# SSD mixer: a chunk's new state from three products of split factors, with the tiles' places shared anew

## The chip, the cores and the metric

The kernel runs on one core of a Trainium2 chip. The metric is the device time of one execution in microseconds. Shown are the median of three runs and, apart from it, one execution that the hardware profiler recorded.

## The reference

One inference step of a two-layer encoder over 512 prompt tokens (one stream) and 8 running streams of 16 tokens, 640 tokens in all, with 1024 channels. Layer 0 is FFN, a mixer of S5 and stick-breaking attention, FFN; layer 1 is FFN, the Mamba-2 SSD mixer, FFN. The change lies in the SSD mixer. Its recurrence, for each of 4 groups of 8 heads (64 channels a head, 128 states), runs over chunks of tokens:

```python
def step(h, inp):
    x_c, dt_c, b_c, c_c = inp
    cs = jnp.cumsum(dt_c * a, axis=1)
    ...
    y = jnp.einsum('btsgr,bsgrp->btgrp', w, x_c)
    y = y + jnp.einsum('btgn,bgrpn->btgrp', c_c, h) * jnp.exp(cs)[..., None]
    to_end = jnp.exp(cs[:, -1:] - cs) * dt_c
    h_new = h * jnp.exp(cs[:, -1])[..., None, None] + jnp.einsum('bsgr,bsgn,bsgrp->bgrpn', to_end, b_c, x_c)
    return h_new, y
```

The last einsum, the sum over a chunk's tokens of B times the scaled x, is the product that the change rewrites. The prompt's state starts at zero; the running streams bring their states with them (`ssd_h0`).

## The kernel before

All is float32 in memory. The big products are made from operands split in two: `split` (lines 99 to 101) casts a value on ScalarE to the type fp32r (the high part) and subtracts that from the value on VectorE (the low part); `mm3` (140 to 148) then sums high x high, low x high and high x low, three fp32r matmuls in place of one. Line 146 is that matmul for most of the kernel. A matmul whose operands are plain float32 shows as two records in the trace.

The SSD mixer (`mixer1`) first projects group 0, then takes 20 steps: 4 groups g, in each the chunks c = 4, 0, 1, 2, 3. Chunk 4 holds the eight running streams; chunks 0 to 3 are 128 prompt tokens each. One turn of the loop at lines 1842 to 1850 issues: one unit of the next group's projections (`run_fill`, line-146 matmuls), `core_a` of the next step, `core_b` (c < 4) or `core_s` (c = 4) of this step, perhaps one more unit, and `gate_out` of the group before.

- `core_a` (1658 to 1719) loads the chunk's B, C and x (`bx`, line 1660, two places) and the running sums (`csb`, 1665), makes the decay weights, transposes B into `bk` (1692, 1698) and x (1701), and scales the transposed x by head: `xe` (factor to the chunk's end) and `xd` (time step), eight ScalarE multiplications each at line 1709 (in group 3, `xd` in one VectorE instruction, 1705). For c = 4 it also splits `xe` and `bk` into `xs_` (a place of `h0`, or of `og` in group 0) and `bs_`, and writes both to DRAM (`xb_d`, 1717 and 1718) for use in the last FFN.
- `core_b` (1721 to 1754): the old state's part (1727), the state product `pst` from `bk` and `xe` (1731), the new state `hst` (1736, 1737), the chunk's own part (1745), and `y` (1749 to 1752). Line 1752 is the last reader of `bx`.
- `core_s` (1756 to 1780): for the running streams, the chunk's own part (1764); then four blocks j of two streams each: `load_h0` (1454 to 1457) brings 512 KB of states, and two matmuls (1769) write 32 rows of the bank `pi`. `xe` is reused for the sum of both (1771, 1772), which is transposed (1775) and finished at 1778, there the last reader of `bx`. Tiles `h0` have four places, and group 0's four loads are issued long before (1825, list `ahead`).

Each tile name has as many places as its `bufs`; a new tile of that name waits until the last reader of the oldest is done. All loads and stores named here are issued by SyncE's queue (SP), in its order. The order on each engine is fixed when the kernel is built: a planner takes the program's order as priority and lets a later instruction pass one that is not ready in its own estimate of times, so that loads and matmuls of a later part can stand ahead of an earlier one in the trace. The trace leaves the numbers out of names: `h0` is `h` there, and all PSUM tiles are `bank`.

Of the kernel before, what the change touches and what calls it, by code (L numbers as in the profile page):

```python
# [10 lines left out]
F32 = mybir.dt.float32  # L11
F32R = mybir.dt.float32r
# [10 lines left out]
T = 640  # L23
# [14 lines left out]
def kernel(ctx: ExitStack, tc: tile.TileContext, I, O, phases=PHASES):  # L38
    nc = tc.nc
# [59 lines left out]
    def split(hi, lo, src):  # L99
        nc.scalar.copy(hi, src)  # L100
        return nc.vector.tensor_tensor(lo, src, hi.bitcast(F32), op=ALU.subtract)  # L101
# [1350 lines left out]
    ssd = {}  # L1452

    def load_h0(wk, g, j):
        h0 = wk.tile([128, 2, 512], F32, name="h0", bufs=4)
        nc.sync.dma_start(h0, I["ssd_h0"][g, 2 * j:2 * j + 2].rearrange("b n c -> n b c"))
        return h0

# [38 lines left out]
    def mixer1(ph, last):  # L1497
# [4 lines left out]
        xb_d = ssd["xb"] = [dram.tile([2, 128, 640], F32, name=f"xb_d{g}") for g in range(4)]  # L1502
        z_d = [dram.tile([128, NT, 4, 128], F32, name=f"z_d{g}") for g in range(4)]
        with ExitStack() as st:
# [105 lines left out]
            nc.sync.dma_start(dr[:, 0:256], I["m1_dt"])  # L1610
            split(dtw[:, 0, 0:256], dtw[:, 1, 0:256], dr[:, 0:256])
            tok = wk.tile([128, NT, 3, 32], F32, name="tok")
            dt, cs = (wk.tile([32, T], F32, name=n) for n in ("dt", "cs"))
            rst, te = (wk.tile([128, 1024], F32, name="csb", bufs=2)[:32, :T] for _ in range(2))
            with after_norm():
                V.memset(rst, 1.0)
# [38 lines left out]
            bl = {}  # L1655
            ahead = []

            def core_a(g, c):
                bx = wk.tile([128, 6, 128], F32, name="bx", bufs=2)
                nc.sync.dma_start(bx, bcx_d[g][:, c])  # L1660
                bt, ct, xs = bx[:, 0], bx[:, 1], bx[:, 2:6]
                hs = slice(8 * g, 8 * g + 8)
                off = lambda r: cs_d[r:r + 1, 128 * c:128 * c + 128].offset
                csb = wk.tile([128, 1024], F32, name="csb", bufs=2).rearrange("p (h t) -> p h t", t=128)
                nc.sync.dma_start(csb, bass.AP(tensor=cs_d.tensor, offset=off(8 * g), ap=[[0, 128], [T, 8], [1, 128]]))

                el = None
                if c < 4:
                    el = small.tile([128, 8], F32, name="el")
                    nc.scalar.activation(el, csb[:, :, 127], AF.Exp)  # L1670
                else:
                    e8 = wk.tile([128, 8, 8], F32, name="e8")
                    nc.scalar.activation(e8.rearrange("p b h -> p h b"),
                                         csb.rearrange("p h (b i) -> p h b i", i=16)[:, :, :, 15], AF.Exp)
                    nc.sync.dma_start(el_d[:, g], e8.rearrange("p b h -> p (b h)"))
                ecs = None
                if 0 < c < 4:
                    ecs = wk.tile([128, 4, 128], F32, name="ecs", bufs=1)
                    for h in range(2):
                        nc.sync.dma_start(ecs[64 * h:64 * h + 64],  # L1680
                                          bass.AP(tensor=cs_d.tensor, offset=off(8 * g + h),
                                                  ap=[[0, 64], [2 * T, 4], [1, 128]]))
                    nc.scalar.activation(ecs, ecs, AF.Exp)
                elif c == 4:
                    ecs = wk.tile([128, 8], F32, name="ecs8")
                    nc.scalar.activation(ecs, tok[:, c, 0, hs], AF.Exp)
                V.tensor_tensor(csb, csb, tok[:, c, 0, hs, None].to_broadcast([128, 8, 128]), op=ALU.subtract)
                nc.scalar.activation(csb, csb, AF.Relu, scale=-1.0)
                nc.scalar.activation(csb, csb, AF.Exp, scale=-1.0)
                pcb = bank_b()  # L1690
                nc.tensor.matmul(pcb[:, 0:128], bt, ct, start=True, stop=True)
                nc.tensor.transpose(pcb[:, 128:256], bt, ident)
                cbm = wk.tile([128, 128], F32, name="cbm", bufs=2)
                V.tensor_tensor(cbm, pcb[:, 0:128], mc[:, c // 4, :], op=ALU.mult)
                V.tensor_tensor(csb, csb, cbm[:, None, :].to_broadcast([128, 8, 128]), op=ALU.mult)

                bk = wk.tile([128, 128], F32, name="bk", bufs=2)
                nc.scalar.copy(bk, pcb[:, 128:256])
                px = bank_b()
                for q in range(4):  # L1700
                    nc.tensor.transpose(px[:, 128 * q:128 * q + 128], xs[:, q], ident)
                xd, xe = (wk.tile([128, 512], F32, name=n, bufs=2) for n in ("xd", "xe"))
                for o, k in ((xe, 2), (xd, 1)):
                    if g == 3 and k == 1:
                        V.tensor_tensor(by_head(o), by_head(px), tok[:, c, k, hs, None].to_broadcast(hb3), op=ALU.mult)
                    else:
                        for h in range(8):
                            d = slice(64 * h, 64 * h + 64)
                            nc.scalar.mul(o[:, d], px[:, d], tok[:, c, k, 8 * g + h:8 * g + h + 1])
                if c == 4:  # L1710

                    xs_ = (wk.tile([128, 2, 512], F32R, name="h0", bufs=4) if g else
                           wk.tile([128, 4, 2, 128], F32R, name="og", bufs=1).rearrange("p (a q) k c -> p a (q k c)", a=2))
                    bs_ = wk.tile([128, 2, 128], F32R, name="bs", bufs=1)
                    split(xs_[:, 0], xs_[:, 1], xe)
                    split(bs_[:, 0], bs_[:, 1], bk)
                    nc.sync.dma_start(xb_d[g][:, :, 0:512].rearrange("a t c -> t a c"), xs_.bitcast(F32))
                    nc.sync.dma_start(xb_d[g][:, :, 512:640].rearrange("a t c -> t a c"), bs_.bitcast(F32))
                bl[g, c] = ct, xs, csb, el, ecs, bk, xd, xe

            def core_b(g, c):
                ct, xs, csb, el, ecs, bk, xd, xe = bl.pop((g, c))

                if c:
                    pi = bank_b().rearrange("p (q t) -> p q t", t=128)
                    for q in range(4):
                        nc.tensor.matmul(pi[:, q, :], hst[g][:, 128 * q:128 * q + 128], ct,
                                         start=(q == 0), stop=(q == 3), skip_group_check=True)

                pst = bank_b()  # L1730
                nc.tensor.matmul(pst, bk, xe, start=True, stop=True)
                hn = wk.tile([128, 512], F32, name="hst", bufs=2)
                if c == 0:
                    nc.scalar.copy(hn, pst)
                else:
                    G.tensor_tensor(by_head(hn), by_head(hst[g]), el[:, :, None].to_broadcast(hb3), op=ALU.mult)
                    V.tensor_tensor(hn, hn, pst, op=ALU.add)
                hst[g] = hn
                if c == 3:
                    nc.sync.dma_start(O["ssd_p"][g], hn)  # L1740

                pw = bank_b().rearrange("p (q t) -> p q t", t=128)
                for q in range(4):
                    for h in range(2):
                        nc.tensor.matmul(pw[64 * h:64 * h + 64, q, :], xd[:, 128 * q + 64 * h:128 * q + 64 * h + 64],
                                         csb[:, 2 * q + h, :], start=(q == 0), stop=(q == 3), skip_group_check=True)
                y = wk.tile([128, 4, 128], F32, name="yb", bufs=6)
                if c:
                    V.tensor_tensor(y, pi, ecs, op=ALU.mult)
                    V.tensor_tensor(y, y, pw, op=ALU.add)  # L1750
                for q in range(4):
                    V.scalar_tensor_tensor(y[:, q, :], xs[:, q], chp[:, 0, 4 * g + q:4 * g + q + 1],
                                           y[:, q, :] if c else pw[:, q, :], op0=ALU.mult, op1=ALU.add)
                ys[g, c] = y

            def core_s(g, c):

                ct, xs, csb, el, ecs, _, xd, xe = bl.pop((g, c))
                c4 = ct.rearrange("p (j q i) -> p j q i", q=2, i=16)
                for q in range(2):  # L1760
                    G.tensor_copy(ctm[:, q, :, q, :], c4[:, :, q, :])
# [90 lines left out]
            for c in range(NT):  # L1852
                gate_out(3, c)
                if c == 0:
                    g_bc = [wk.tile([128, 2, 512], F32, name="h0", bufs=4).rearrange("p a b -> p (a b)")
                            for _ in range(2)]
                    load_gb(LN_OF[ph], g_bc)
                layer_norm(c, g_bc, last)
                if c >= 2:
                    run_pend()  # L1860
# [159 lines left out]
```

## Time and profile before

| | |
|---|---|
| median of 3 runs | 2525.61 us (2523.7 to 2527.52) |
| profiled execution, own time | 2531.27 us |
| its span, first to last instruction | 2529.6 us |
| mean granted TensorE clock | 0.995 of full |
| busy: TensorE, VectorE, ScalarE, GpSimd | 2490.1, 2014.5, 1269.2, 373.5 us |
| line 1731, the state product | 16 products, 32 records, 594 ns each |
| line 1769, the running streams' states | 64 records in 4 steps |

The recurrence of the SSD mixer spans about 1660 to 2050 us of the trace. The page gives busy time by engine, and the views of groups of instructions (by line and shape), of waits (who waited for whom), of stretches of time and of single engines in order of time give the rest. Busy shares of TensorE overstate its work, since matmuls overlap: a group's time from its first start to the next group's start is what it costs. In the view in order of time a row gives the start, the length from first start to last end, the engine, line and operation, and the number of instructions merged; a bracket gives the idle time before it and what ended that.

### The profile page before, as it was taken

How to read it: one execution, taken by the hardware profiler on the slowest of the kernel's cores; microseconds unless marked ns; L12 is line 12 of the kernel's file. 1: busy time of each engine (PE TensorE's matmuls, PEld its weight loads, DVE VectorE, ACT ScalarE, POOL GpSimd, SP SyncE). 2: the span in 40 equal slices, each digit the busy share in tenths (PEclk: the TensorE clock that was granted, in tenths of full speed). 3: DMA queues.
4: the chain of work that ended last, by engine and by line, in shares of the span. 5: the costliest groups of instructions: out<-in, count | busy, mean ns of one | idle time of the engine just before them, and what ended most of it. 6: DMA issues, size and time to landing. Idle time of an engine off the chain costs nothing. (4 is left out here: it accounts for less than half of the span.)

```text
span 2529.6 us, 40802 instructions
## 1 busy us (share of the span) xinstructions
PE 2490.1 (98%) x15551; PEld 2286.1 (90%) x15551; DVE 2014.5 (80%) x3505; ACT 1269.2 (50%) x2389; POOL 373.5 (15%) x492
## 2 busy tenths in 40 slices
PE   9999999999999999999999999999999999999998
PEld 8999999878789999999999999998999879999897
DVE  7788777676879888877988887787575789998887
ACT  4444344336744555553555554566465543554542
POOL 0000001210130000013000002311121152111121
PEclk9999999999999999999999999999999999999999
DMA  5332335443222433452144434556464723555563
GB/s 186 109 100 78 116 112 161 144 150 117 87 79 64 119 102 97 112 164 66 59 114 113 120 100 132 158 162 204 137 211 137 242 74 99 154 151 165 151 172 116
DMA packets 179253, 324.80 MB, mean 128 GB/s; under 512 B 21312, under 2 KB 92608, under 8 KB 178544
## 3 DMA queue, kind: packets, MB, share of 16 engines
q1 hardware_dynamic: 165200, 293.83, 36.9%
q0 software_dynamic: 13856, 28.35, 5.8%
q8 instruction: 122, 2.00, 0.3%
q14 instruction: 75, 0.61, 0.1%
HBM read 259.56 MB, written 40.54 MB: 119 GB/s over the span
## 5 line engine op out<-in xcount | busy, mean ns | idle before, releaser
L100 ACT CAST w<-raw 128x512 fp32r<-128x512 f32 (+1 forms) x721 | 532.7, 769 | 337.3 <-DVE raw L349 144.7
L101 DVE TENSOR_TENSOR w<-raw,w 128x512 fp32r<-128x512 f32 (+2 forms) x721 | 621.2, 883 | 86.9 <-ACT w L100 84.0
L366 PE MATMUL bank<-xhi,w 128*128 128x320 f32 x2432 | 436.2, 309 | 2.3 <-DVE s L408 1.4
L366 PE MATMUL bank<-T,w 128*128 128x320 f32 x2736 | 428.2, 310 | 5.3 <-ACT bank L383 2.7
L366 PEld LDWEIGHTS bank<-T,w 128*128 128x128 f32 x2736 | 406.8, 188 | 8.6 <-ACT bank L383 5.3
L366 PEld LDWEIGHTS bank<-xhi,w 128*128 128x128 f32 x2432 | 376.8, 188 | 6.6 <-DVE s L408 2.2
L146 PE MATMUL bank<-xhi,w 128*128 128x256 f32 (+2 forms) x2272 | 364.3, 312 | 5.2 <-ACT xhi L100 2.6
L146 PEld LDWEIGHTS bank<-xhi,w 128*128 128x128 f32 x2272 | 337.3, 189 | 15.8 <-issue 4.9
L146 PE MATMUL bank<-w,h 128*128 128x512 f32 x1488 | 346.5, 391 | 0.2 <-DVE yacc L223 0.2
L146 PEld LDWEIGHTS bank<-w,h 128*128 128x128 f32 x1488 | 277.2, 188 | 57.9 <-ACT h L100 1.6
L366 PE MATMUL bank<-xlo,w 128*128 128x320 f32 x1216 | 227.8, 309 | 0.0
L349 DVE TENSOR_TENSOR raw<-raw 128x512 f32<-128x512 f32 x304 | 214.0, 704 | 3.4
L366 PEld LDWEIGHTS bank<-xlo,w 128*128 128x128 f32 x1216 | 190.8, 188 | 0.0
L146 PE MATMUL bank<-xlo,w 128*128 128x256 f32 (+2 forms) x1136 | 190.0, 309 | 0.0
L515 POOL DMA_DIRECT2D yacc<-ev x84 | 72.6, 893 | 690.2 <-ACT ev L514 619.8
L146 PEld LDWEIGHTS bank<-xlo,w 128*128 128x128 f32 x1136 | 171.6, 188 | 0.6
L502 PE MATMUL bank<-w,h 128*128 128x512 f32 x576 | 134.5, 390 | 0.0
L502 PEld LDWEIGHTS bank<-w,h 128*128 128x128 f32 x576 | 107.9, 188 | 22.7 <-DVE yacc L511 0.2
L379 ACT COPY mx<-bank 128x320 f32<-128x320 f32 x152 | 64.6, 425 | 105.9 <-PE bank L366 105.2
L223 DVE SCALAR_TENSOR_TENSOR yacc<-bank,yacc 128x512 f32<-128x512 f32 x120 | 82.0, 687 | 40.3 <-PE bank L146 39.7
L511 DVE SCALAR_TENSOR_TENSOR yacc<-bank,yacc 128x512 f32<-128x512 f32 x84 | 57.8, 688 | 67.4 <-PE bank L502 67.4
L146 PE MATMUL bank<-w,og 128*128 128x512 f32 x432 | 103.1, 394 | 0.0
(437 smaller groups left out, 3359.0 us busy)
## 6 DMA issues: line engine op xcount, KB each, us to landing
raw<-in_w_gate_dram SPq DMA_DIRECT2D x88, 512.0 KB, 3.7
raw<-in_w_up_dram SPq DMA_DIRECT2D x88, 512.0 KB, 3.8
raw<-in_w_down_dram SPq DMA_DIRECT2D x88, 512.0 KB, 3.6
raw<-in_m_in_dram SPq DMA_DIRECT2D x52, 512.0 KB, 4.6
yacc<-ev POOLq DMA_DIRECT2D x84, 256.0 KB, 4.7
raw<-in_m_out_dram SPq DMA_DIRECT2D x24, 512.0 KB, 4.3
csb<-cs_d SPq DMA_DIRECT2D x20, 512.0 KB, 5.3
h<-in_ssd_h_dram SPq DMA_DIRECT2D x16, 512.0 KB, 6.6
```

The lines of the kernel that those rows point to most:

```text
L100: nc.scalar.copy(hi, src)
L101: return nc.vector.tensor_tensor(lo, src, hi.bitcast(F32), op=ALU.subtract)
L146: state["pe"] = nc.tensor.matmul(ps, a, b, start=(k == 0), stop=(k == n - 1)).ins
L223: state["acc"] = nc.vector.scalar_tensor_tensor(ya, pb, scale, ya, op0=ALU.mult, op1=ALU.add).ins
L349: V.tensor_tensor(o, v, w, op=ALU.subtract)
L366: nc.tensor.matmul(ps, A[p][:, a, k * 128:k * 128 + 128], X[p][b][:, k, :], start=(first and n == 0), stop=(n == 11), skip_group_check=True)
L379: nc.scalar.copy(e[n], ps)
L502: nc.tensor.matmul(ps, a[:, u], b[:, v], start=(first and n == 0), stop=(n == 5), skip_group_check=True)
L511: V.scalar_tensor_tensor(ya, ps, 0.5 / ALPHA, ya, op0=ALU.mult, op1=ALU.add)
L515: nc.gpsimd.dma_start(yacc[:, t, 512 * j:512 * j + 512], e, accum_op=ALU.add)
```

## The change

The state product's factors are split for every chunk, and line 1731 becomes three fp32r matmuls into the same bank: high x high, high x low, low x high. `bk` and `xe` hold both parts; `xe` is first made whole in a new tile `xr` with one place, split, and only then is `xd` made. For c = 4 the parts that exist now go to DRAM, and `xs_` and `bs_` go. `core_s` takes `xr` for the sum that it kept in `xe`. To make room, `h0` has three places, not four, and `dt`, used only ahead of the loop, lies in the place of `og`.

```diff
     def load_h0(wk, g, j):
-        h0 = wk.tile([128, 2, 512], F32, name="h0", bufs=4)
+        h0 = wk.tile([128, 2, 512], F32, name="h0", bufs=3)
...
-            dt, cs = (wk.tile([32, T], F32, name=n) for n in ("dt", "cs"))
+            dt = wk.tile([128, 4, 2, 128], F32, name="og", bufs=1).rearrange("p q k c -> p (q k c)")[:32, :T]
+            cs = wk.tile([32, T], F32, name="cs")
...
-                bk = wk.tile([128, 128], F32, name="bk", bufs=2)
-                nc.scalar.copy(bk, pcb[:, 128:256])
+                bk = wk.tile([128, 2, 128], F32R, name="bk", bufs=2)
+                split(bk[:, 0], bk[:, 1], pcb[:, 128:256])
...
-                xd, xe = (wk.tile([128, 512], F32, name=n, bufs=2) for n in ("xd", "xe"))
-                for o, k in ((xe, 2), (xd, 1)):
+                xd = wk.tile([128, 512], F32, name="xd", bufs=2)
+                xr = wk.tile([128, 512], F32, name="xr", bufs=1)
+                xe = wk.tile([128, 2, 512], F32R, name="xe", bufs=2)
+                for o, k in ((xr, 2), (xd, 1)):
...
+                    if k == 2:
+                        split(xe[:, 0], xe[:, 1], xr)
                 if c == 4:
-
-                    xs_ = (wk.tile([128, 2, 512], F32R, name="h0", bufs=4) if g else
-                           wk.tile([128, 4, 2, 128], F32R, name="og", bufs=1).rearrange("p (a q) k c -> p a (q k c)", a=2))
-                    bs_ = wk.tile([128, 2, 128], F32R, name="bs", bufs=1)
-                    split(xs_[:, 0], xs_[:, 1], xe)
-                    split(bs_[:, 0], bs_[:, 1], bk)
-                    nc.sync.dma_start(xb_d[g][:, :, 0:512].rearrange("a t c -> t a c"), xs_.bitcast(F32))
-                    nc.sync.dma_start(xb_d[g][:, :, 512:640].rearrange("a t c -> t a c"), bs_.bitcast(F32))
+                    nc.sync.dma_start(xb_d[g][:, :, 0:512].rearrange("a t c -> t a c"), xe.bitcast(F32))
+                    nc.sync.dma_start(xb_d[g][:, :, 512:640].rearrange("a t c -> t a c"), bk.bitcast(F32))
...
                 pst = bank_b()
-                nc.tensor.matmul(pst, bk, xe, start=True, stop=True)
+                for n, (a, b) in enumerate(((0, 0), (0, 1), (1, 0))):
+                    nc.tensor.matmul(pst, bk[:, a], xe[:, b], start=(n == 0), stop=(n == 2))
...
-                ct, xs, csb, el, ecs, _, xd, xe = bl.pop((g, c))
+                ct, xs, csb, el, ecs, _, xd, _ = bl.pop((g, c))
+                xe = wk.tile([128, 512], F32, name="xr", bufs=1)
...
-                    g_bc = [wk.tile([128, 2, 512], F32, name="h0", bufs=4).rearrange("p a b -> p (a b)")
+                    g_bc = [wk.tile([128, 2, 512], F32, name="h0", bufs=3).rearrange("p a b -> p (a b)")
```

## The prediction

> **What bounds the kernel now.** I read the page first, then the stretches of time, then TensorE's waits in the SSD mixer, then the mixer's engines in order of time.
>
> ```profile
> PE 2490.1 (98%) x15551; PEld 2286.1 (90%) x15551; DVE 2014.5 (80%) x3505; ACT 1269.2 (50%) x2389; POOL 373.5 (15%) x492
> ```
>
> ```profile
> 1650.00:2050.00 400.00, 394.69 (x2615) 356.93 (x2615) 285.15 (x485) 234.14 (x622) 77.59 (x149) 0.99 0.57 176
> 1756.00:1759.50 3.50, 1.08 (x7) 0.76 (x5) 2.69 (x4) 1.75 (x4) 0.00 (x0) 1.00 0.95 288
> 1759.50:1769.70 10.20, 10.12 (x46) 7.10 (x47) 6.09 (x9) 5.84 (x23) 0.51 (x4) 0.50 0.65 203
> ```
>
> The columns of the stretches are its length, the busy time of TensorE, its weight loads, VectorE, ScalarE and GpSimd, then the granted clock, DMA's share and GB/s. TensorE is busy for 394.69 of the mixer's 400 us; VectorE for 285.15 (71%) and ScalarE for 234.14 (59%). So what lengthens or shortens TensorE's stream counts in full, and work on the other two counts only where TensorE waits for it. The other two rows show the worst such place: TensorE stood still from 1757.08 (1755.53 + 1.55, below) to 1759.58, and the next 10.2 us were granted half the clock.
>
> ```profile
> 1755.53 1.55 PE L146 MATMUL bank<-xlo,w 128*128 128x384 f32 x8
> 1759.58 0.77 PE L1691 MATMUL bank<-bx 128*128 128x128 f32 x2 [2.50 <-DMA bx<-bcx_d]
> ...
> 2020.69 0.46 PE L1691 MATMUL bank<-bx 128*128 128x128 f32 x2 [0.67 <-DMA bx<-bcx_d]
> ...
> 2031.82 0.49 PE L1691 MATMUL bank<-bx 128*128 128x128 f32 x2 [0.39 <-DMA bx<-bcx_d]
> ```
>
> That place costs 2.5 us of waiting and half of 10.2, 5.1 us: 7.6 us. With the two waits at the end these are all three of TensorE's waits for `bx` in 20 loads; the other 17 steps had it in time.
>
> **The change part by part.** *The state product.* In the views by shape (busy us, mean ns) and in order of time:
>
> ```profile
> L146 PE MATMUL bank<-w,og 128*128 128x512 f32 x384 | 91.7, 394 | 0.0
> ...
> L1731 PE MATMUL bank<-xe,bk 128*128 128x512 f32 x32 | 16.4, 594 | 0.0
> ```
>
> ```profile
> 2012.09 1.02 PE L1731 MATMUL bank<-xe,bk 128*128 128x512 f32 x2
> ...
> 2014.31 5.71 PE L146 MATMUL bank<-w,og 128*128 128x512 f32 x24
> ...
> 2026.76 1.02 PE L1731 MATMUL bank<-xe,bk 128*128 128x512 f32 x2
> 2027.46 3.97 PE L146 MATMUL bank<-w,og 128*128 128x512 f32 x16
> ```
>
> One product is two records of 594 ns in 1.02 us together, so the second starts 0.43 us after the first and the pair takes 0.86 us of the stream. The new matmuls have the type and shape of the 24 at 2014.31; without the last one's own 0.39 us the other 23 starts fill 5.32 us, (5.71 - 0.39)/23 = 0.231 us each (the group of 16: (3.97 - 0.39)/15 = 0.239), their weight loads included. Three take 0.69 us. Over 16 products: 16 x (0.86 - 0.69) = **-2.7 us** (-2.3 with 0.239). A switch between types seems to cost nothing: at 2026.76 a plain product stands between fp32r matmuls, and the next starts 0.70 us on, not later than 0.86.
>
> The Trainium skill, "TensorE: Matmul & The Clock Gate", section "Back-to-back issue gap", gives about 131 ns for each 512-column matmul in a sustained stream; by it three would take 0.39 us and the change save 7.5 us, an estimate. The rows here disagree, with 231 to 239 ns, and the measurement decides.
>
> *The fourth `h0` load.* This is the part that I think matters most. Four blocks of the running streams' states used to have four places. With three, the fourth block's load can start only when the first block's matmuls are done.
>
> ```profile
> 1671.55 1.94 PE L1769 MATMUL bank<-h,ctm 128*32 128x512 f32 x16
> 1673.43 2.10 PE L146 MATMUL bank<-xhi,w 128*128 128x256 f32 x16
> 1675.36 1.07 PE L146 MATMUL bank<-xlo,w 128*128 128x256 f32 x8
> 1676.27 0.33 PE L146 MATMUL bank<-xhi,w 128*128 128x384 f32 x1
> 1676.44 0.60 PE L1775 MATMUL bank<-ident,xe 128*128 128x128 f32 x4
> 1676.80 2.85 PE L146 MATMUL bank<-xhi,w 128*128 128x384 f32 x15
> ```
>
> ```profile
> 1671.55 0.18 PEld L1769 LDWEIGHTS bank<-h,ctm 128*32 128x32 f32 x8
> 1672.01 0.15 PEld L1769 LDWEIGHTS bank<-h,ctm 128*32 128x32 f32 x4 [0.28 <-issue]
> 1672.44 0.15 PEld L1769 LDWEIGHTS bank<-h,ctm 128*32 128x32 f32 x4 [0.28 <-issue]
> ```
>
> Sixteen records of 512 columns, 4 for each block, go through in 1.88 us (1671.55 to 1673.43): the weight loads come in fours, 0.43 us apart, so the four blocks, each 32 columns wide, run side by side in four steps. If the fourth must come later, the first three still take four steps and so does the fourth alone: 1.88 us more (four bare steps, 1.72, at least), in each of 4 groups: **+7.5 us** (6.9 at least; 0 if the planner found a way to keep them together, which a place still in use seems to exclude). A fill of projections follows, so the fourth block has something to stand behind, as the transposes at 1676.44 stand inside a group of line 146.
>
> ```profile
> L1456 SPq DMA_DIRECT2D h<-in_ssd_h_dram x16: 368/467/846, 1594.9 to 1979.1; - x16
> ...
> DMA to landing us min/median/max: 4.4/6.6/8.8
> ```
>
> The load lands 4.4 to 8.8 us after its issue, and the planner puts the matmuls where it expects that. Where it expects too little, TensorE waits. The nearest rows are its three waits for `bx`, loads with as little lead: 0.39, 0.67 and 2.50. I take the middle one: 4 x 0.67 = **+2.7 us** (0 to 10). `bx` of this step is released later by as much (line 1778), but outside group 0 the next load has some 10 us to spare: issued at 1773.79, it is read at 1789.20.
>
> ```profile
> 1773.79 0.32 SPq L1660 DMA_DIRECT2D bx<-bcx_d  x1
> ```
>
> ```profile
> 1789.20 0.38 PE L1691 MATMUL bank<-bx 128*128 128x128 f32 x2
> ```
>
> *The splits.* Sixteen more of `xe` and of `bk` than before:
>
> ```profile
> L101 DVE TENSOR_TENSOR h<-xe,h 128x512 fp32r<-128x512 f32 x3 | 2.1, 687 | 0.0
> L101 DVE TENSOR_TENSOR bs<-bk,bs 128x128 fp32r<-128x128 f32 x4 | 1.1, 285 | 0.0
> L100 ACT CAST h<-xe 128x512 fp32r<-128x512 f32 x3 | 2.2, 732 | 0.0
> ```
>
> VectorE gets 16 x (0.687 + 0.285) = 15.5 us, to 75% of the stretch; ScalarE some 16 x 0.73 = 11.7 us, to 61% (the casts of `bk` stand in for its copies). `core_a` runs a step ahead of `core_b`, so both are hidden, and so is the one place of `xr`, free again as soon as a split is done. Without that cover each step would pay up to 0.97 us. The cover is thin only in group 3's last steps, where no fill is left and TensorE already waits: 0 to 2.9 us for three steps; I take one of the three, **+1.0 us**. `dt` in `og`'s place and the later gains in `h0` cost nothing: `og` is first wanted steps after `dt` is read, and `h0` is idle by then.
>
> *The place at 1757.* SP, ScalarE and VectorE ahead of it:
>
> ```profile
> 1751.99 0.37 SPq L1586 DMA_DIRECT2D bcx_d<-acc  x1
> 1752.45 0.46 SPq L1717 DMA_DIRECT2D xb_d<-h  x1
> 1753.00 0.44 SPq L1718 DMA_DIRECT2D xb_d<-bs  x1
> 1753.53 1.13 SPq L1660 DMA_DIRECT2D bx<-bcx_d  x1
> ```
>
> ```profile
> 1746.62 1.81 ACT L1709 ACTIVATE xd<-bank,tok 128x64 f32<-128x64 f32 x8
> 1748.18 0.76 ACT L100 CAST h<-xe 128x512 fp32r<-128x512 f32 x1
> ```
>
> ```profile
> bx<-bcx_d SPq DMA_DIRECT2D x20, 384.0 KB, 4.1
> xb_d<-h SPq DMA_DIRECT2D x3, 512.0 KB, 3.7
> ```
>
> `bx` took 6.05 us from issue to use, against a median of 4.1 to landing, with DMA 95% busy. Just ahead of it in the queue went the `xb_d` stores of 512 and 128 KB, and they were late because the split stood behind the `xd` multiplications (1.81 us). The change splits before `xd`, so these stores can go ahead of line 1586, and one of the four state loads around `bx` moves to after the matmuls. With 4.1 us `bx` lands at 1757.6, and half a microsecond of the wait is left. That is too little to halve the clock by what this trace shows: waits of 0.39 and 0.67 did not. So -2.0 and -5.1: **-7.1 us**.
>
> The sum: -2.7 + 7.5 + 2.7 + 1.0 - 7.1 = **+1.4 us**. The profiled execution's own 2531.27 (span 2529.6) becomes 2532.7; the median is 5.66 lower, so 2525.61 becomes **2527.0 us**. About 0.2%, 5.1 us, is what a measurement can tell from no change; this is within it.
>
> **The rivals.**
>
> *The gap at 1757 stays.* If the planner leaves the stores where they are, or the later load's place in the queue only shifts the crowd, the -7.1 goes: +8.5, 2534.1 us. For it: line 1660 also waits for the last reader of its place on VectorE (among SP's waits, total, times, longest), which the change doesn't bring forward.
>
> ```profile
> SPq L1660 <- DVE yb L1752: 18.1, 11, 2.9
> ```
>
> Against it: the two causes named above.
>
> *The fourth load comes too late (slower).* One wait like that at 1757, 2.5 us and not 0.67, adds 1.8 and halves the clock for 5.1: +6.9 a place, so 2533.9 for one and 2540.8 for two of four. It decides from where the load's landing exceeds the plan by about 2.5 us; the range of 4.4 to 8.8 allows it, a single load without three others beside it speaks against it. The Trainium skill, the same page, "Why this matters for your kernels", sets the limit at idle gaps over about 3 us; by that rule one such wait would cost 1.8 us alone. The trace is stricter: 2.5 us sufficed.
>
> *The fourth block costs nothing (faster).* If the planner runs the first block early enough for the fourth to join the other two, 7.5 and 2.7 fall away: -8.8, 2516.8 us, or -1.7, 2523.9, if the gap stays too. For it: the blocks depend on little but the load. Against it: before, all four stood after line 1764 in program order.
>
> *The change doesn't do what it says.* If fp32r matmuls between plain ones run no faster (0.86 in all), +2.7: 2529.7 us.
>
> **How the numbers follow.** Forecast 0.40; gap stays 0.21; too late 0.18; costs nothing 0.16 (0.12 of it with the gap closed); no saving 0.05. Faster by over 0.2% are the 0.12 and 0.03 of the forecast's lower end: 0.15. Slower are 0.19 of the gap's case, 0.16 of the late load's and 0.04 of the forecast's upper end: 0.39. The rest, 0.46, is within. The forecast's own range is 2522 to 2531; to hold 8 in 10, it reaches to 2541 for up to two late places and to 2517 for the cheap fourth block: 2517 to 2541.
>
> **What would show it.** Line 1731 with 48 records, three in 0.69 us of the stream; line 1769 in two groups for each g, of 12 and 4 records, each about 1.8 us, with projections between; in TensorE's waits a row with `h` as releaser, under 3 us in all; the clock at 1.00 through the place at 1757. I am wrong if the 16 records stay together, if the clock is halved at a fourth load, or if VectorE or ScalarE becomes what TensorE waits for in the middle steps.

## The result and the profile after

The changed kernel takes 2537.45 us (median of 6 runs, 2534.16 to 2541.55) against 2524.69 us (6 runs) for the kernel before: a ratio of 1.0047, 95% interval 1.0036 to 1.0058. That is 12.8 us slower, more than the noise. The forecast of no measurable change (2527.0) missed it by 10.4 us; its range (2517 to 2541) held the time. The recorded execution took 2536.05 us (span 2534.3 us).

The product and the fourth blocks first, by shape (busy us, mean ns):

```profile
L1770 PE MATMUL bank<-h,ctm 128*32 128x512 f32 x64 | 15.9, 607 | 7.9 <-DMA h<-in_ssd_h_dram 7.9
L1731 PE MATMUL bank<-xe,bk 128*128 128x512 f32 x48 | 15.0, 420 | 0.0
```

Line 1731 has 48 records now, of 420 ns for 594. Line 1770 is line 1769 of before; in front of it TensorE stood still for 7.9 us, and in order of time one sees where:

```profile
1670.45 1.93 PE L1770 MATMUL bank<-h,ctm 128*32 128x512 f32 x12
1672.31 2.10 PE L146 MATMUL bank<-xhi,w 128*128 128x256 f32 x16
1674.24 1.07 PE L146 MATMUL bank<-xlo,w 128*128 128x256 f32 x8
1675.15 0.85 PE L146 MATMUL bank<-xhi,w 128*128 128x384 f32 x4
1677.41 1.90 PE L1770 MATMUL bank<-h,ctm 128*32 128x512 f32 x4 [1.41 <-DMA h<-in_ssd_h_dram]
1679.24 2.36 PE L146 MATMUL bank<-xhi,w 128*128 128x384 f32 x12
...
1768.47 1.90 PE L1770 MATMUL bank<-h,ctm 128*32 128x512 f32 x4 [1.82 <-DMA h<-in_ssd_h_dram]
...
1882.99 1.90 PE L1770 MATMUL bank<-h,ctm 128*32 128x512 f32 x4 [1.64 <-DMA h<-in_ssd_h_dram]
...
1998.04 2.44 PE L1770 MATMUL bank<-h,ctm 128*32 128x512 f32 x4 [3.05 <-DMA h<-in_ssd_h_dram]
```

Twelve records of three blocks fill 1.86 us of the stream (1670.45 to 1672.31), where sixteen filled 1.88 before; the fourth block's four fill another 1.83 (1677.41 to 1679.24). Each of the four late groups waits for its load. The loads were issued here, the fourth block's as the first of each row:

```profile
1672.38 1.40 SPq L1456 DMA_DIRECT2D h<-in_ssd_h_dram  x3
...
1763.20 2.24 SPq L1456 DMA_DIRECT2D h<-in_ssd_h_dram  x3
...
1877.22 0.89 SPq L1456 DMA_DIRECT2D h<-in_ssd_h_dram  x2
...
1991.02 0.38 SPq L1456 DMA_DIRECT2D h<-in_ssd_h_dram  x1
```

From issue to use they took 5.0, 5.3, 5.8 and 7.0 us. TensorE was free for them (the group's start less its wait) 3.5 to 4.1 us after the issue. The last wait fell in a crowd, and the clock was halved after it; the stretches of time (TensorE, its weight loads, VectorE, ScalarE, GpSimd, clock, DMA share, GB/s):

```profile
1650.00:2050.00 400.00, 388.94 (x2581) 350.04 (x2579) 291.37 (x502) 237.86 (x627) 69.23 (x138) 1.00 0.58 177
1756.00:1759.50 3.50, 3.50 (x26) 3.50 (x24) 3.38 (x5) 1.49 (x5) 0.00 (x0) 1.00 0.51 161
...
1994.00:1999.30 5.30, 2.25 (x9) 1.02 (x8) 0.42 (x1) 0.37 (x1) 0.00 (x0) 1.00 1.00 357
1999.30:2002.70 3.40, 3.40 (x9) 2.29 (x8) 2.12 (x3) 0.22 (x1) 0.00 (x0) 0.50 0.46 166
```

TensorE stood still for 11.1 us of the mixer's 400, against 5.3 before. The place at 1757 is full and at full clock. From 1994 to 1999.3 the DMA engines were 100% busy and TensorE was not.

Since every step of the loop begins with the same matmul of `core_a` (line 1691, now 1692), the differences of its starts in order of time tell where the time went. Steps are named by the `core_a` that begins them; "before again" is a second recording of the kernel before (below), "four places" the first experiment.

```
us                                    before  before again    after  four places
(0,0), holds core_s of group 0         18.79         18.79    22.33        20.20
(1,4), the wait at 1757                20.18         19.68    17.35        17.35
(1,0), holds core_s of group 1         29.62         25.67    28.57        25.45
(2,0), holds core_s of group 2         24.88         25.12    28.36        24.65
(3,0), holds core_s of group 3         24.68         24.68    31.36        24.79
11 other steps, (0,1) to (3,4)        224.20        224.20   222.01       222.04
(3,1) to the mixer's last gate         65.98         68.11    66.89        66.50
all else                             2121.22       2117.53  2117.46      2116.75
span                                 2529.6        2523.8   2534.3       2517.7
```

Against the second recording the changed kernel loses 3.54 + 2.90 + 3.24 + 6.68 = 16.4 us in the four steps with `core_s`, gains 2.3 at the wait ahead of step (1,0), 2.2 in the eleven plain steps and 1.2 at the end: 10.5 us in all. The gain at the end is none of the change's: in the second recording the clock was halved there for 3.4 us (2032.2 to 2035.6), 1.7 us. Against the first recording, with the full clock there, the changed kernel's end takes 0.9 us more.

### The profile page after: what moved, and what is told of

It is laid out like the page before. It is cut to its first block, busy times and chain, and to the rows that moved or that the text cites. A ratio compares the mean times of both kernels' runs of the same rounds, so it can differ in the third digit from the quotient of the medians.

```text
span 2534.3 us, 40880 instructions
## 1 busy us (share of the span) xinstructions
PE 2490.7 (98%) x15567; PEld 2283.7 (90%) x15567; DVE 2026.5 (80%) x3537; ACT 1278.5 (50%) x2401; POOL 374.2 (15%) x492
```

## The experiments

Theory 1: the lost place of `h0` is the cost, in two parts, the fourth block alone (7.5 us) and the wait for its load. Theory 2: the added splits on ScalarE and VectorE are. And one question for one of the prediction's two largest terms: does the halved clock at 1757 belong to the kernel, or to the one execution that was recorded? The kernel before ran beside all of them; its medians were 2526.28, 2525.69 and 2526.46 us in the three sets (23, 15 and 29 runs).

**Four places again** (`cs`, read only ahead of the loop, goes into a place of `h0`; `bufs=4` at `g_bc` too):

```diff
-        h0 = wk.tile([128, 2, 512], F32, name="h0", bufs=3)
+        h0 = wk.tile([128, 2, 512], F32, name="h0", bufs=4)
...
-            cs = wk.tile([32, T], F32, name="cs")
+            cs = wk.tile([128, 2, 512], F32, name="h0", bufs=4).rearrange("p a b -> p (a b)")[:32, :T]
...
```

> The changed kernel with four places for h0 again; room is made by putting cs (read only ahead of the loop) in a place of h0. Theory 1 (the lost place of h0 is the cost: the fourth block runs alone, 4 x 1.88 us, and TensorE waits for its load, 7.9 us): 2521 to 2526 us, the 16 records of line 1770 together again and no wait for h. Theory 2 (the added splits on ScalarE and VectorE are the cost): it stays at 2534 to 2540 us.

2519.64 us (7 runs), ratio to before 0.9975 (0.9964 to 0.9986): 6.6 us faster than before, 17.8 faster than the changed kernel, a little more than theory 1 gave (2521 to 2526). All splits are in it, so theory 2 can't be the loss. TensorE in order of time, the group whole again:

```profile
1669.46 1.94 PE L1770 MATMUL bank<-h,ctm 128*32 128x512 f32 x16
```

This version is faster than both kernels.

**The fourth block later.** Three places, but the matmuls of block 3 follow a whole unit of projections:

```diff
                 for j in range(4):
                     h0 = ahead.pop(0) if ahead else load_h0(wk, g, j)
+                    if j == 3:
+                        run_fill(1)
+                    with tc.issue_after(state["pe"]) if j == 3 else ExitStack():
...
-                run_fill(0 if i in (8, 14) else 1)
+                run_fill(0 if i in (8, 14) or c == 4 else 1)
```

> The changed kernel, three places, but the fourth block's two matmuls stand behind a whole further unit of projections, so that its load has time. Theory 1 splits its cost in two, and this takes the wait alone away: 7.9 us of waiting and 1.7 us of halved clock less than 2537.5, so 2526 to 2531 us, with the four records still in a group of their own. Rival: the wait only moves to the next load that is then late (bx, which is released later), and the time stays above 2534 us.

2530.03 us (11 runs), ratio 1.0013 (1.0004 to 1.0022). The groups stay apart, with no wait for `h` between:

```profile
1669.43 1.93 PE L1773 MATMUL bank<-h,ctm 128*32 128x512 f32 x12
...
1678.38 1.90 PE L1773 MATMUL bank<-h,ctm 128*32 128x512 f32 x4
```

So this order brings 7.4 us (2537.45 to 2530.03). The waits and the halved clock that went were 9.6 us in the recorded execution (7.9 and 1.7); in group 3 a wait of 2.1 us for the sum in `xr` came in their place:

```profile
PE bank L1779 <- DVE xr L1776: 2.1, 1, 2.1
```

The rest of the lost place is some 10 us (to 2519.64), of which the blocks alone are 7.3 (4 x 1.83); the remaining 3 are not taken apart here.

**One plain product for the three**, all splits kept; it leaves out the low parts. First with four places, then with three:

```diff
-                for n, (a, b) in enumerate(((0, 0), (0, 1), (1, 0))):
-                    nc.tensor.matmul(pst, bk[:, a], xe[:, b], start=(n == 0), stop=(n == 2))
+                nc.tensor.matmul(pst, bk[:, 0].bitcast(F32), xe[:, 0].bitcast(F32), start=True, stop=True)
```

> As the first of these kernels, but the state product is one plain float32 matmul of the two high parts (read as float32); it leaves out the low parts. All splits stay. Theory 1 (three products take 0.69 us of the stream where one plain takes 0.86): 2.7 us slower than with three products. Rival (the saving is lost at the changes of type around them, as 872 against 955 ns from the first start to line 1745 hints): at most 1.3 us slower, or no difference.

> The changed kernel (three places) with one plain product of the high parts for the three; it leaves out the low parts. With four places that cost 10.1 us where the steps without waits gave 0.16 us each, 2.6 in all. If the rest was the planner's other order of that one kernel, here the difference to 2537.5 is another, 2 to 6 us: 2539 to 2544. Rival (a plain product really costs 10 us more): 2546 to 2549.

2529.76 us with four places (11 runs, ratio 1.0012, 1.0004 to 1.0021), 10.1 more than with three products; 2543.07 us with three (5 runs, 1.0071, 1.0057 to 1.0085), 5.6 more. The plain steps are 0.16 us longer each (17.51 for 17.35), as in the kernel before; over sixteen products that would make 2.6. The rest lies elsewhere and differs between the two, so it is not the product's own price. Both wait at the end of the mixer, where the kernels with three products don't (TensorE's waits: total, times, longest; the first two rows are of four places, the last of three):

```profile
PE bank L1799 <- POOL zz L1798: 4.4, 2, 3.4
PE bank L1775 <- DVE xr L1772: 4.0, 2, 2.9
```

```profile
PE bank L1799 <- POOL zz L1798: 4.5, 2, 3.4
```

With four places the recorded executions differ by 9.5 us. The plain steps and the wait ahead of step (1,0) give 1.7 of them, step (1,0) 2.4, with a wait of 2.87 us for the sum in `xr`. The end gives 3.7, of which 1.7 is a clock halved for 3.4 us right behind the wait (2023.6 to 2027.0). Some 1.5 lie outside the mixer. With three places the wait for `h` in group 1 was 4.87 us, and the clock was halved for 6.8 us behind it.

**High x high alone**, with four places (it leaves out both other products):

```diff
-                for n, (a, b) in enumerate(((0, 0), (0, 1), (1, 0))):
-                    nc.tensor.matmul(pst, bk[:, a], xe[:, b], start=(n == 0), stop=(n == 2))
+                nc.tensor.matmul(pst, bk[:, 0], xe[:, 0], start=True, stop=True)
```

> As the kernel with four places of h0, but the state product is the high x high matmul alone; it leaves out the two others. If each of these matmuls costs its 0.23 us of the stream: the steps without waits are 2 x 0.23 = 0.46 us shorter, and the median 16 x 0.46 = 7.3 us below 2519.6, 2511 to 2514. Rival (the work is hidden, and the 10.1 us between one plain and three fp32r products came from elsewhere): less than 3 us.

2519.71 us (11 runs, ratio 0.9974, 0.9965 to 0.9983): nothing gained on 2519.64. Yet the plain steps did shrink as expected, by 0.46 us (17.35 to 16.89):

```profile
1704.02 0.38 PE L1692 MATMUL bank<-bx 128*128 128x128 f32 x2
...
1720.91 0.38 PE L1692 MATMUL bank<-bx 128*128 128x128 f32 x2
...
1737.81 0.38 PE L1692 MATMUL bank<-bx 128*128 128x128 f32 x2
```

In the recorded execution the eleven plain steps and the one ahead of step (1,0) are 5.5 us shorter than with three products. The `core_s` steps take 1.7 more, the end of the mixer 2.4, and all else 4.0. The same wait stands at the end:

```profile
PE bank L1799 <- POOL zz L1798: 5.1, 2, 4.1
```

Behind it the clock was halved for 3.4 us, and once more outside the mixer (2230.0 to 2233.4): 1.7 us each, which the recording with three products has at neither place. So a product's price shows in full in the steps without waits, and is lost again in others, to waits and the clock behind them. The order of the last steps is another with one product than with three. Why it comes out worse there stays open, and so do the other 2.3 us outside the mixer in this one execution.

**The kernel before, recorded again:**

> The kernel before, unchanged, recorded once more. If the halved clock at 1757 belonged to the one execution that was recorded first (2531.27 us against a median of 2524.69), this one takes 2522 to 2527 us, with the clock whole there. If it belongs to the kernel, the clock is halved again and the execution takes about 2525 with it, or 2531.

2525.49 us. Ahead of step (1,0) it waits 2.0 us, and the next 10 us have the full clock:

```profile
1756.99 0.46 PE L1691 MATMUL bank<-bx 128*128 128x128 f32 x2 [2.00 <-DVE acc L1578]
```

```profile
1757.00:1767.00 10.00, 10.00 (x75) 7.89 (x76) 7.30 (x11) 7.04 (x25) 2.01 (x4) 1.00 0.85 267
```

Of the 67 executions of the kernel before that ran beside the experiments, two had a mean clock of 0.995 like the one recorded first, and they took 2530.5 and 2531.7 us; the 25 with 0.996 took 2528.5 on average, the 22 with 0.998 took 2524.5. As much halved clock as in the first recording was rare; where it lay in the others is not on record. The two other kernels below that keep this wait (1.70 and 1.75 us) had the full clock there too.

**The changed kernel, recorded again:**

> The changed kernel, unchanged, recorded once more: four waits of TensorE for h between 1 and 4 us, 6 to 10 us in all, also where the clock is not halved; 2534 to 2541 us. If the 7.9 us were an accident of one execution, they are under 4 us here and the time is near 2531.

2541.73 us, again with four waits, of 0.55 to 3.01 us; here the clock was halved twice in the mixer, after 1681 and after 2002 us, for 3.4 us each.

```profile
PE bank L1770 <- DMA h<-in_ssd_h_dram: 8.4, 4, 3.0
```

**The kernel before with three places** and nothing else (`bufs=4` to `bufs=3` at the three tiles named `h0`):

> The kernel before with three places of h0 and nothing else changed. Theory 1 (the lost place): slower by what the changed kernel lost by it, 7.5 us for four blocks alone and 5 to 10 us of waiting, so 2536 to 2545 us, line 1769 in groups of 12 and 4 records or fewer. Theory 2 (the splits, or the order of the new tiles): within 3 us of 2526.

2538.56 us (5 runs), ratio 1.0049 (1.0037 to 1.0062): 12.9 us slower, about what the whole change loses. The waits are there too:

```profile
PE bank L1769 <- DMA h<-in_ssd_h_dram: 6.6, 3, 2.5
PE bank L1691 <- DMA bx<-bcx_d: 2.5, 3, 1.7
```

So the lost place is enough for such a loss without any other part of the change. That the two totals agree is chance: here no product is cheaper and the wait ahead of step (1,0) stays, `xs_` takes one of the three places in groups 1 to 3, and group 3's fourth block waits for nothing.

**The early split in the kernel before**, for the wait ahead of step (1,0): the block with `xs_` and `bs_` moves ahead of the `xd` multiplications.

```diff
                             nc.scalar.mul(o[:, d], px[:, d], tok[:, c, k, 8 * g + h:8 * g + h + 1])
+                    if c == 4 and k == 2:
...
+                        split(xs_[:, 0], xs_[:, 1], xe)
+                        split(bs_[:, 0], bs_[:, 1], bk)
...
```

> The kernel before, all else as it was, but for c = 4 the split of xe and bk stands ahead of the xd multiplications, as in the changed kernel. If the late split and stores make the wait for bx ahead of step (1,0): the step that takes 19.7 to 20.2 us before comes down to 17.5, and the median by some 2 us, to 2523 to 2524.5. Rival (what goes is the crowd of state loads around bx): that step keeps some 19.5 us.

2527.72 us (12 runs), ratio 1.0009 (1.0001 to 1.0017), and the step keeps 19.43 us. The large store does go earlier (SP, VectorE and TensorE of this kernel):

```profile
1745.18 0.36 SPq L1717 DMA_DIRECT2D xb_d<-h  x1
...
1751.06 0.33 SPq L1660 DMA_DIRECT2D bx<-bcx_d  x1
```

```profile
1749.89 1.14 DVE L1752 SCALAR_TENSOR_TENSOR yb<-bx,chp,yb 128x128 f32<-128x128 f32 x4
```

```profile
1738.81 1.09 PE L1745 MATMUL bank<-csb,xd 128*64 128x128 f32 x16
...
1755.63 0.46 PE L1691 MATMUL bank<-bx 128*128 128x128 f32 x2 [1.75 <-DMA bx<-bcx_d]
```

`bx` is issued at 1751.06 because line 1752, its place's last reader, ends at 1751.03 on VectorE, 12.2 us after line 1745 of that chunk begins. With four places and the whole change the same interval is 9.3 us, and nothing waits:

```profile
1748.84 1.14 DVE L1752 SCALAR_TENSOR_TENSOR yb<-bx,chp,yb 128x128 f32<-128x128 f32 x4
```

```profile
1740.68 1.09 PE L1745 MATMUL bank<-csb,xd 128*64 128x128 f32 x16
...
1755.58 0.38 PE L1692 MATMUL bank<-bx 128*128 128x128 f32 x2
```

So the early stores alone don't close the gap, and fewer places alone don't either (19.4 us in the kernel above). What goes with the closed gap is an earlier line 1752 on VectorE; why the planner's order brings it there is open.

**Plain factors in group 3.** With four places, chunks 0 to 3 of group 3 keep the plain product of whole factors and no split:

```diff
+                whole = g == 3 and c < 4
+                if whole:
+                    nc.scalar.copy(bk[:, 0].bitcast(F32), pcb[:, 128:256])
...
+                xr = xe[:, 0].bitcast(F32) if whole else wk.tile([128, 512], F32, name="xr", bufs=1)
...
```

> Four places of h0 as in the first kernel, but in group 3 the prompt's four chunks keep the plain product of whole factors, with no split, since there TensorE waits for ScalarE and VectorE (og, xr, bk) with no projections left to stand behind. If the splits cost at the end of the mixer: 1 to 3 us faster than 2519.6. Rival (the plain product costs 4 x 0.17 us and the splits are hidden there too): 2520 to 2521 us.

2522.69 us (11 runs), ratio 0.9984 (0.9975 to 0.9993): 3 us slower than with the splits everywhere. That doesn't show the splits to be free at the end. The recorded execution takes 67.6 us from step (3,1) to the last gate, but the clock was halved there for 3.4 us (2027.8 to 2031.3), behind waits of 1.15 and 0.70 us. Without these 1.7 us the end takes 65.9, as in the first recording of the kernel before (65.98) and 0.5 less than with the splits (66.50). What is slower besides is step (1,0), by 0.8, and all else, by 1.9 us; why is open.

**The sum of `core_s` in `xd`** and not in `xr`, with four places:

```diff
-                xe = wk.tile([128, 512], F32, name="xr", bufs=1)
+                xe = xd
```

> As the kernel with four places of h0, but core_s sums in its own xd, which line 1765 has read by then, and not in xr. If the single place of xr makes the transposes wait for the sum (1.5 us in two waits, step (0,4) to (0,0) 20.2 us for 18.8 before): 1 to 2 us faster than 2519.6 and that step below 19 us. Rival (VectorE's order, in which line 1688 with its late csb stands ahead of the sum): no difference beyond 1 us.

2520.55 us (12 runs), ratio 0.9982 (0.9973 to 0.999). Step (0,0) falls from 20.20 to 18.95 us, so the single `xr` does cost 1.25 us there; steps (1,0) and (3,1) take 0.8 and 1.2 us more, and the median is no better.

## Where the prediction was right and where wrong

*The state product* was right in its sum: 0.17 us each predicted, 0.16 in the chunks without waits (17.51 to 17.35). The parts are other ones. From the start of the product to that of line 1745 it takes 0.96 us before and 0.88 after, for 0.86 and 0.69; the other 0.08 lies ahead of it: from the start of line 1727 (1726 after) to that of the product 0.89 before and 0.81 after. So part of the agreement is luck.

*The fourth block alone* was right: 7.5 us predicted, 12 and 4 records as described, 7.3 us measured.

*The wait for its load* is the step that failed most. The prediction took 4 x 0.67 = 2.7 us from the middle one of three waits for `bx` (with 0 to 10 as the bounds) and gave "under 3 us in all" as a sign; 7.9 and 8.4 us were measured. The load was as quick as allowed, 5.0 to 7.0 us from issue to use, but what stood ahead of the matmuls lasted only 3.5 to 4.1 us from the issue. Two of the three waits taken as a guide were in the last steps, where little else moves; around the four new ones the same queue had projections' weights, sums or the next group's states, and at the last DMA was at 100%. The rival "the fourth load comes too late" was so partly true: at one place (two in the second recording) a wait of about 3 us halved the clock for 3.4 us, 1.7 us each, where the rival had 5.1. A clock halved at a fourth load was also one of the prediction's own signs of being wrong. In all this term is 9.6 us for 2.7.

*The place at 1757* is the other step that failed. The prediction took 7.1 us off the median, and 5.1 of them were a halved clock that the first recorded execution had there; none of the three other recordings with this wait has it. It even said that this execution was 5.66 us above the median, and carried that difference along as if it were a constant of recording. What the kernel has there is a wait of some 2 us; it did go, 2.2 us (19.68 to 17.51, and 17.35 with the product's 0.16), though not for the reason given: the early stores alone left it. The rival "the gap at 1757 stays" had named what holds `bx` back, line 1752 on VectorE, and thought that the change would not bring it forward; it came earlier.

*The splits* cost nothing that shows in the middle steps. At the end, +1.0 was predicted, and the changed kernel takes 0.9 more there than the first recording of the kernel before (66.89 for 65.98), although its products are cheaper by some 0.5. So the term was about right; that it is the splits is not separated from the new order of these steps. The one place of `xr`, put at nothing, cost 1.25 us in step (0,0) once `h0` had four places.

With the measured terms the sum is -2.6 + 7.3 + 9.6 - 2.2 + 1.4 = +13.5 us (1.4 for the end, 0.9 and the products' 0.5), against 12.8 measured; the terms come from single recorded executions. Of the miss of 11.4 us (12.8 for +1.4), the wait for the load and its clock make 6.9 and the place at 1757 4.9, both to the same side. That the range held is partly luck: its upper part stood for two late loads at 6.9 us each on top of a gap that gave 7.1. The late loads came and were cheaper, and the gap gave only 2.2. With only the clock's 5.1 us left out of the old sum the forecast would have been +6.5, outside what counts as no change.

## What to carry to other kernels

A place taken from a tile that several side-by-side matmuls read together cost twice here: the group broke into two passes of full length, and the second waited for a transfer that could only start when the first was done. Count a tile's places against the largest group that must be alive at once before giving one away; here 2.5 KB from a tile that was dead by then kept the group whole, and the change then gained 6.6 us. And before a term from one recorded execution is set against a median, check that the median can contain it: an execution several us above its median, with a stretch of halved clock of the same worth, is the warning.

## What the runs showed of the hardware

The program lists the matmuls of line 1769 as block 0, block 0, block 1, block 1 and so on, two a block, and a plain product has two records; yet 16 records of four blocks took 1.88 us, 12 of three 1.86, and 4 of one 1.83. Different column blocks so ran side by side, and a block fewer in the group saved nothing. Whether the planner or TensorE set them side by side, the traces, which don't number the blocks, don't show.

The length of a wait did not by itself decide the clock. In these traces of the mixer single waits of up to 2.1 us left it whole, and so did one of 2.87 us (one plain product, four places, ahead of 1769.33). Waits of 2.46 us (the kernel before with three places, 1677.59), 2.50 (before, 1759.58) and 3.05 us (after, 1998.04) were followed by half the clock. So was a pair of 0.99 and 0.70 us at 2031 in the second recording of the kernel before, while the same pair in the first (1.04 and 0.70) was not. So the 2.5 us that the prediction took for the limit is none. The halved stretches lasted 3.4 us, 6.8 us (behind 4.87 us, three places with one plain product) or 10.2 us (before, from 1759.58).
